# Weight loads and a stage's last outputs ahead in the engines' queues, at the seams of a one-core transformer kernel

## Chip, cores and metric

One core of a Trainium2 chip (trn2). The time is device microseconds (us) of one execution of the kernel; less is better. The time before is the median of three runs.

## What is computed

Two blocks on `x` of 512 positions by 1024 channels, in float32. Cut to what matters here:

```python
def _rms_norm(x, g):
    return x * rsqrt(mean(x * x, axis=-1) + EPS) * g

def _swiglu(x, w_gate, w_up, w_down):
    return (silu(x @ w_gate) * (x @ w_up)) @ w_down      # 1024 -> 2816 -> 1024

# first block, layers 0 and 1 (mixer: attention in layer 0, mLSTM in layer 1)
hf = _swiglu(_rms_norm(x, g[0]), ...)
x = x + 0.5 * _rms_norm(hf, g[1])
x = x + _rms_norm(mixer(_rms_norm(x, g[2])), g[3])
hf = _swiglu(_rms_norm(x, g[4]), ...)
x = x + 0.5 * _rms_norm(hf, g[5])

# second block: even mixer (pooling and a state space scan), odd mixer (gated convolution)
x = x + even_mixer(_rmsnorm(x, even_norm))
x = x + odd_mixer(_rmsnorm(x, odd_norm))
return _rmsnorm(x, final_norm)
```

What counts for the change: between two stages there is always a norm over the channels of the stage's output, an addition to x, and a norm of the new x ahead of the next stage.

## The kernel before

**Stages.** The program runs nine stages in a row: ffn0, attn, ffn1, ffn2, mlstm, ffn3, even, odd, and the final norm. Where one stage ends and the next begins is called a seam here. x is held transposed, as eight tiles (`x_91` to `x_98`) of 128 channels by 512 positions; the 512 positions are worked on in two halves of 256 columns, so that the second half's work in one stage runs beside the first half's chain on x.

**Linears.** For precision each linear is three matmuls per tile of 128 input channels (`mm3`, L280 to L290): the weight's low part times the high part of x (L287), the weight's high part times the low part of x (L288), high times high (L289). The high and low parts of x are the tiles `xs_99` to `xs_106`. A weight tile comes by `wload` (L260 to L269): an SP queue DMA into `wt` (L264), a cast into `wh` on ACT (L267), and the subtraction that leaves `wl` on DVE, or on POOL for some linears (L268). Each of the three has four buffers, so a load waits until an older tile's matmuls are done.

**End of a stage.** The last four linears run half by half (`halves`), in an ffn the very last two by `last_two` (L350 to L369), which loads two of the first linear's three weight parts a second time. Each output is evacuated from its PSUM bank on ACT by `PostNorm.evac`: its square into `ew` (L530) and its value times the gain into `yf`, `hn` or `x` (L531). The square is added to `acc` on POOL, the last of a half on DVE (L535). When a half is complete, `finish` starts a chain of small steps for it.

**The chain on x.** Per half: column sums of `acc` by matmuls with ones (L407 acc), the inverse root (`rsv`: DVE L427, POOL L428), its spread over the partitions (L415). Then for each of the eight tiles the output times the root (DVE L551), the addition to x (L553, on DVE, two of eight on POOL), the split into high (ACT L469) and low (DVE L470), the square (ACT L451) and its sum (L453 on DVE and POOL, the last L455 on DVE). Then column sums again (L407 ssq), the inverse root (`rc`: L427, L428), its spread (L415) and a copy (`rb`, L487). The matmuls of the next stage's linears need only the split of x; the factor `rb` is multiplied in when their result leaves its bank (L573 in an ffn, L700 in attn). There are four such banks, so PE can run up to four linears ahead of the end of the chain, and then waits.

**What sets the order.** The Python code yields pieces of the chains between pieces of the linears; a scheduler then gives every engine one queue in fixed order. `k.ahead(n)` raises the priority of what is written inside it, as if it had been written up to n instructions earlier. `k.chains` holds the chains that aren't finished.

Of the kernel before, what the change touches and what calls it, by code (L numbers as in the profile page):

```python
# [9 lines left out]
F32 = mybir.dt.float32  # L10
R = mybir.dt.float32r
AF = mybir.ActivationFunctionType
ALU = mybir.AluOpType
# [6 lines left out]
HALF = 256  # L20
# [121 lines left out]
class K:  # L142
# [60 lines left out]
    def evac(s, f, c0, c1):  # L203

        s.held.append((f, c0, c1))
        s.settle()
# [53 lines left out]
def wload(k, src, shape, eng=None):  # L260

    nc = k.nc
    wt = k.wp.tile(shape, F32, name="wt", tag="wt", bufs=4)
    nc.sync.dma_start(wt, src)  # L264
    wh = k.wp.tile(shape, R, name="wh", tag="wh", bufs=4)
    wl = k.wp.tile(shape, R, name="wl", tag="wl", bufs=4)
    nc.scalar.copy(wh, wt)  # L267
    (eng or nc.vector).tensor_tensor(wl, wt, wh.bitcast(F32), op=ALU.subtract)  # L268
    return wh, wl  # L269


# [21 lines left out]
class Lin:  # L293
# [12 lines left out]
    def load_part(s, i):  # L306
        src, n = s.parts[i]
        s.w[i] = wload(s.k, src, [P, n, P], s.eng)
# [44 lines left out]
def last_two(k, l0, l1, on_half):  # L353


    l0.run(*HALVES[0])
    l1.run(*HALVES[0])
    l0.w = [None, None, l0.w[2]]
    on_half(*HALVES[0])
    ps = k.A_()  # L360
    l0.part(ps, 2, *HALVES[1], True, False)
    with k.ahead(80):
        l0.load_part(0)
    l1.run(*HALVES[1])
    with k.ahead(80):
        l0.load_part(1)
    l0.part(ps, 0, *HALVES[1], False, False)
    l0.part(ps, 1, *HALVES[1], False, True)
    k.evac(lambda: l0.evac(ps, *HALVES[1]), *HALVES[1])  # L369
    on_half(*HALVES[1])  # L370


class LinTok:
# [5 lines left out]
    def run(s, tb):  # L379
        if s.w is None:  # L380
            s.w = [wload(s.k, s.src[:, 2 * kc:2 * kc + 2, :], [P, 2, T], s.eng) for kc in range(4)]
        mm = s.k.nc.tensor.matmul
        s.k.need("xs", tb * P, (tb + 1) * P)
        ps = s.k.A_()
        t = slice(tb * P, (tb + 1) * P)
        for i in range(KX):
            wh, wl = s.w[i // 2]
            xh, xl = s.xs[i]
            mm(ps, xl[:, t], wh[:, i % 2, :], start=i == 0, stop=False)
            mm(ps, xh[:, t], wl[:, i % 2, :], start=False, stop=False)  # L390
            mm(ps, xh[:, t], wh[:, i % 2, :], start=False, stop=i == KX - 1)
            s.k.tick()
        s.k.evac(lambda: s.evac(tb, ps), tb * P, (tb + 1) * P)
# [121 lines left out]
class PostNorm:  # L515
# [7 lines left out]
    def evac(s, m):  # L523
        def f(ps, c0, c1):
            k, nc = s.k, s.k.nc
            first, last = s.acc is None, c1 - c0 < T and len(s.done[c0]) == KX - 1
            if first:
                s.acc = k.sm.tile([P, T], F32, name="acc", tag="acc", bufs=1)
            sq = s.acc if first else k.ew()
            nc.scalar.activation(sq[:, c0:c1], ps[:, c0:c1], AF.Square)  # L530
            nc.scalar.activation(s.hf[m][:, c0 // HALF:c1 // HALF, :], ps[:, c0:c1].rearrange("p (a t) -> p a t", t=HALF),  # L531
                                 AF.Copy, scale=s.gain[:, m:m + 1])
            if not first:
                eng = nc.vector if last else nc.gpsimd
                eng.tensor_tensor(s.acc[:, c0:c1], s.acc[:, c0:c1], sq[:, c0:c1], op=ALU.add)  # L535
            for a, b in HALVES:
                if c0 <= a and b <= c1:
                    s.done[a].append(m)
        return f
# [18 lines left out]
def ffn(k, w, gpost, side=None, begin=None):  # L558
# [4 lines left out]
    with k.phase("ffn") as pool, k.psum("ffn_ps", True), ExitStack() as late:  # L563
# [57 lines left out]
        for m in range(KX):  # L621
            src = k.A["wd"][w, m]
            lins.append(Lin(k, [(src[:, a:b], b - a) for a, b in ((0, 8), (8, 16), (16, 22))], hs, post.evac(m)))
        run_lins(lins[:-2])
        last_two(k, *lins[-2:], post.finish)


# [1024 lines left out]
```

## Time and profile before

| | |
|---|---|
| median of three runs | 2566.19 us (2565.17 to 2567.06) |
| profiled execution | 2566.05 us |
| its span | 2564.3 us |
| mean granted clock of TensorE | 0.987 of full speed |
| PE busy | 2465.5 us, 96% of the span |
| DVE busy | 1363.8 us, 53% |
| ACT busy | 1000.4 us, 39% |
| POOL busy | 634.1 us, 25% |

PE is TensorE, DVE is VectorE, ACT ScalarE, POOL GpSimd, SP SyncE, whose queue issues the loads. The profile is of one execution; its times are us from the start of the span. Busy shares are means over all stages; a seam is a few us of 2564.

### The profile page before, as it was taken

How to read it: one execution, taken by the hardware profiler on the slowest of the kernel's cores; microseconds unless marked ns; L12 is line 12 of the kernel's file. 1: busy time of each engine (PE TensorE's matmuls, PEld its weight loads, DVE VectorE, ACT ScalarE, POOL GpSimd, SP SyncE). 2: the span in 40 equal slices, each digit the busy share in tenths (PEclk: the TensorE clock that was granted, in tenths of full speed). 3: DMA queues.
4: the chain of work that ended last, by engine and by line, in shares of the span. 5: the costliest groups of instructions: out<-in, count | busy, mean ns of one | idle time of the engine just before them, and what ended most of it. 6: DMA issues, size and time to landing. Idle time of an engine off the chain costs nothing. (4 is left out here: it accounts for less than half of the span.)

```text
span 2564.3 us, 33234 instructions
## 1 busy us (share of the span) xinstructions
PE 2465.5 (96%) x12960; PEld 2072.1 (81%) x12960; DVE 1363.8 (53%) x2298; ACT 1000.4 (39%) x1659; POOL 634.1 (25%) x560
## 2 busy tenths in 40 slices
PE   8999999999999999999999999999899999999897
PEld 7888887677888888888888888888788888787677
DVE  5344247656544432643422567558963246856885
ACT  5222235446532222422222454453222233346662
POOL 2111013030311110211100344032211015317961
PEclk9999999999999999999999999999999999999898
DMA  4323324122232333222233222223433345231211
GB/s 160 99 99 102 116 87 145 50 87 66 76 106 99 98 121 101 84 99 99 97 123 101 87 83 75 74 71 123 161 130 122 97 133 201 84 112 66 66 50 58
DMA packets 90125, 256.85 MB, mean 100 GB/s; under 512 B 16192, under 2 KB 25024, under 8 KB 89456
## 3 DMA queue, kind: packets, MB, share of 16 engines
q1 hardware_dynamic: 89968, 254.73, 31.1%
q8 instruction: 102, 1.67, 0.3%
q14 instruction: 55, 0.45, 0.1%
HBM read 229.50 MB, written 12.60 MB: 94 GB/s over the span
## 5 line engine op out<-in xcount | busy, mean ns | idle before, releaser
L287 PE MATMUL pa<-xs,wl 128*128 128x512 f32 (+1 forms) x2304 | 864.5, 375 | 25.2 <-DVE identr L243 7.9
L288 PE MATMUL pa<-xs,wh 128*128 128x512 f32 (+1 forms) x2304 | 861.7, 374 | 0.8 <-DVE xs L1423 0.6
L289 PE MATMUL pa<-xs,wh 128*128 128x512 f32 (+1 forms) x2304 | 859.6, 373 | 0.0
L267 ACT CAST wh<-wt 128x1024 fp32r<-128x1024 f32 (+2 forms) x418 | 428.0, 1025 | 978.4 <-issue 581.6
L268 DVE TENSOR_TENSOR wl<-wt,wh 128x1024 fp32r<-128x1024 f32 (+1 forms) x374 | 454.7, 1216 | 436.8 <-ACT wh L267 435.7
L287 PEld LDWEIGHTS pa<-xs,wl 128*128 128x128 f32 x2304 | 437.9, 190 | 101.8 <-ACT xs L469 13.8
L288 PEld LDWEIGHTS pa<-xs,wh 128*128 128x128 f32 x2304 | 437.9, 190 | 74.8 <-DVE xs L1423 2.5
L289 PEld LDWEIGHTS pa<-xs,wh 128*128 128x128 f32 x2304 | 438.0, 190 | 74.0 <-issue 1.8
L575 POOL TENSOR_TENSOR ew<-ew,rb 128x512 f32<-128x512 f32 (+1 forms) x96 | 159.9, 1666 | 724.9 <-ACT ew L574 724.9
L287 PE MATMUL pa<-hh,wl 128*128 128x512 f32 (+1 forms) x880 | 309.0, 351 | 4.1 <-DVE wl L268 4.1
L289 PE MATMUL pa<-hh,wh 128*128 128x512 f32 (+1 forms) x880 | 307.9, 350 | 0.0
L288 PE MATMUL pa<-hl,wh 128*128 128x512 f32 (+1 forms) x880 | 307.9, 350 | 0.0
L535 POOL TENSOR_TENSOR acc<-acc,ew 128x512 f32<-128x512 f32 (+1 forms) x46 | 56.9, 1238 | 548.3 <-ACT ew L530 548.0
L287 PEld LDWEIGHTS pa<-hh,wl 128*128 128x128 f32 x880 | 165.5, 188 | 29.1 <-DVE wl L268 4.9
L288 PEld LDWEIGHTS pa<-hl,wh 128*128 128x128 f32 x880 | 165.5, 188 | 24.3
L582 DVE TENSOR_TENSOR ew<-ew,pa 128x512 f32<-128x512 f32 (+1 forms) x96 | 61.6, 642 | 232.1 <-PE pa L289 223.1
L289 PEld LDWEIGHTS pa<-hh,wh 128*128 128x128 f32 x880 | 165.5, 188 | 23.9
L573 DVE TENSOR_TENSOR ew<-rb,pa 128x512 f32<-128x512 f32 (+1 forms) x96 | 61.6, 642 | 173.1 <-PE pa L289 172.2
L268 POOL TENSOR_TENSOR wl<-wt,wh 128x1024 fp32r<-128x1024 f32 x44 | 106.7, 2437 | 111.2 <-ACT wh L267 111.1
L1505 POOL TENSOR_TENSOR tp<-tp 128x512 f32<-128x512 f32 x72 | 99.9, 1388 | 5.1 <-ACT tp L1501 0.7
L1512 DVE SCALAR_TENSOR_TENSOR pc<-g,vecs,pc 128x512 f32<-128x512 f32 x120 | 85.8, 751 | 5.4 <-PE pc L1510 4.3
L469 ACT ACTIVATE xs<-x,vecs 128x256 fp32r<-128x256 f32 x128 | 61.0, 504 | 61.1 <-DVE x L553 41.3
(516 smaller groups left out, 2967.5 us busy)
## 6 DMA issues: line engine op xcount, KB each, us to landing
wt<-in_wgu_dram SPq DMA_DIRECT2D x176, 512.0 KB, 3.5
wt<-in_wd_dram SPq DMA_DIRECT2D x72, 512.0 KB, 3.5
wt<-in_wd_dram SPq DMA_DIRECT2D x32, 384.0 KB, 3.1
wt<-in_ow_dram SPq DMA_DIRECT2D x24, 512.0 KB, 3.2
wt<-in_aqk_dram SPq DMA_DIRECT2D x18, 512.0 KB, 4.0
xs<-x SPq DMA_DIRECT2D x32, 256.0 KB, 2.3
wt<-in_mvo_dram SPq DMA_DIRECT2D x16, 512.0 KB, 3.7
wt<-in_mqk_dram SPq DMA_DIRECT2D x16, 512.0 KB, 3.2
```

Of the source, the lines that this page charges most:

```text
L267: nc.scalar.copy(wh, wt)
L268: (eng or nc.vector).tensor_tensor(wl, wt, wh.bitcast(F32), op=ALU.subtract)
L287: mm(ps[:m, c0:c1], wl[:, j, :], xh[:, c0:c1], start=first and j == 0, stop=False)
L288: mm(ps[:m, c0:c1], wh[:, j, :], xl[:, c0:c1], start=False, stop=False)
L289: mm(ps[:m, c0:c1], wh[:, j, :], xh[:, c0:c1], start=False, stop=last and j == n - 1)
L469: nc.scalar.activation(xh[:, c0:c1], k.x[i][:, c0:c1], AF.Copy, scale=k.vec(g, i))
L535: eng.tensor_tensor(s.acc[:, c0:c1], s.acc[:, c0:c1], sq[:, c0:c1], op=ALU.add)
L573: nc.vector.tensor_tensor(s[:, c0:c1], rb[:, c0:c1], ps[:, c0:c1], op=ALU.mult)
L575: nc.gpsimd.tensor_tensor(s[:, c0:c1], s[:, c0:c1], rb[:, c0:c1], op=ALU.mult)
L582: nc.vector.tensor_tensor(s[:, c0:c1], s[:, c0:c1], ps[:, c0:c1], op=ALU.mult)
L1505: nc.gpsimd.tensor_tensor(part, part, t, op=ALU.add)
L1512: nc.vector.scalar_tensor_tensor(ps, gi[:, j:j + T], cw[:, at[j]:at[j] + 1], ps, op0=ALU.mult, op1=ALU.add)
```

## The change

Three edits. In `wload`, what is issued for a weight tile (the DMA, the cast, the subtraction) gets `k.ahead(250)` while a chain is unfinished, and stays at its place otherwise. In `last_two`, the `ahead(80)` around the two loads goes, since `wload` has its own now. In `PostNorm.evac`, the square, the scaled value and the addition to `acc` get `ahead(250)` while a chain is unfinished.

```diff
 def wload(k, src, shape, eng=None):
 
     nc = k.nc
-    wt = k.wp.tile(shape, F32, name="wt", tag="wt", bufs=4)
-    nc.sync.dma_start(wt, src)
-    wh = k.wp.tile(shape, R, name="wh", tag="wh", bufs=4)
-    wl = k.wp.tile(shape, R, name="wl", tag="wl", bufs=4)
-    nc.scalar.copy(wh, wt)
-    (eng or nc.vector).tensor_tensor(wl, wt, wh.bitcast(F32), op=ALU.subtract)
+    with k.ahead(250 if k.chains else 0):
+        wt = k.wp.tile(shape, F32, name="wt", tag="wt", bufs=4)
+        nc.sync.dma_start(wt, src)
+        wh = k.wp.tile(shape, R, name="wh", tag="wh", bufs=4)
+        wl = k.wp.tile(shape, R, name="wl", tag="wl", bufs=4)
+        nc.scalar.copy(wh, wt)
+        (eng or nc.vector).tensor_tensor(wl, wt, wh.bitcast(F32), op=ALU.subtract)
     return wh, wl
...
     l0.part(ps, 2, *HALVES[1], True, False)
-    with k.ahead(80):
-        l0.load_part(0)
+    l0.load_part(0)
     l1.run(*HALVES[1])
-    with k.ahead(80):
-        l0.load_part(1)
+    l0.load_part(1)
...
             sq = s.acc if first else k.ew()
-            nc.scalar.activation(sq[:, c0:c1], ps[:, c0:c1], AF.Square)
-            nc.scalar.activation(s.hf[m][:, c0 // HALF:c1 // HALF, :], ps[:, c0:c1].rearrange("p (a t) -> p a t", t=HALF),
-                                 AF.Copy, scale=s.gain[:, m:m + 1])
-            if not first:
-                eng = nc.vector if last else nc.gpsimd
-                eng.tensor_tensor(s.acc[:, c0:c1], s.acc[:, c0:c1], sq[:, c0:c1], op=ALU.add)
+            with k.ahead(250 if k.chains else 0):
+                nc.scalar.activation(sq[:, c0:c1], ps[:, c0:c1], AF.Square)
+                nc.scalar.activation(s.hf[m][:, c0 // HALF:c1 // HALF, :],
+                                     ps[:, c0:c1].rearrange("p (a t) -> p a t", t=HALF), AF.Copy, scale=s.gain[:, m:m + 1])
+                if not first:
+                    eng = nc.vector if last else nc.gpsimd
+                    eng.tensor_tensor(s.acc[:, c0:c1], s.acc[:, c0:c1], sq[:, c0:c1], op=ALU.add)
```

The lines of the changed kernel from 264 to 362 stand one lower in the file than before (L268 is L269), those from some 366 to 528 one higher (L407 is L406, L427 is L426, L455 is L454).

No instruction of PE, DVE, POOL or SP comes or goes; ACT has three loads of its function tables less, all in ffn3's first part. Only the seams and the kernel's start have a new order. Two places:

DVE at the seam from attn to ffn1, from the splits of the last two x tiles of the first half (`xs6_105`, `xs7_106`) to the second half's chain. The four `wl` are the first four weight tiles of ffn1, `rsv` belongs to the second half, `rc` to the first. Before:

```order
L470 SCALAR_TENSOR_TENSOR xs6_105<-x6_97,vecs_89,xs6_105 128x256
L453 TENSOR_TENSOR ssq_5550<-ssq_5550,sq_5558 128x256
L470 SCALAR_TENSOR_TENSOR xs7_106<-x7_98,vecs_89,xs7_106 128x256
L453 TENSOR_TENSOR ssq_5550<-ssq_5550,sq_5561 128x256
L268 TENSOR_TENSOR wl_5696<-wt_5693,wh_5695 128x1024
L455 TENSOR_TENSOR ssq_5550<-ssq_5550,ssq_5542 128x256
L268 TENSOR_TENSOR wl_5804<-wt_5801,wh_5803 128x1024
L535 TENSOR_TENSOR acc_5221<-acc_5221,ew_5655 128x256
L268 TENSOR_TENSOR wl_5846<-wt_5843,wh_5845 128x1024
L427 TENSOR_SCALAR rsv_5712<-pb_5709 128x2
L427 TENSOR_SCALAR rc_5470<-pb_5721 128x2
L268 TENSOR_TENSOR wl_5881<-wt_5878,wh_5880 128x1024
```

and with the change, from the last of the four `wl` on:

```order
L269 TENSOR_TENSOR wl_5881<-wt_5878,wh_5880 128x1024
L553 TENSOR_TENSOR x7_98<-x7_98,ew_5537 128x256
L452 TENSOR_TENSOR ssq_5550<-ssq_5550,sq_5552 128x256
L535 TENSOR_TENSOR acc_5221<-acc_5221,ew_5655 128x256
L452 TENSOR_TENSOR ssq_5550<-ssq_5550,sq_5555 128x256
L469 SCALAR_TENSOR_TENSOR xs6_105<-x6_97,vecs_89,xs6_105 128x256
L426 TENSOR_SCALAR rsv_5712<-pb_5709 128x2
L469 SCALAR_TENSOR_TENSOR xs7_106<-x7_98,vecs_89,xs7_106 128x256
L452 TENSOR_TENSOR ssq_5550<-ssq_5550,sq_5558 128x256
L452 TENSOR_TENSOR ssq_5550<-ssq_5550,sq_5561 128x256
L454 TENSOR_TENSOR ssq_5550<-ssq_5550,ssq_5542 128x256
L426 TENSOR_SCALAR rc_5470<-pb_5721 128x2
```

All four `wl`, the second half's last addition to `acc` and its `rsv` now stand ahead of the first half's last step on `ssq` (L455, now L454). On PE the column sums of `acc` stood behind `xs_103`'s matmuls with those of `ssq` right behind them and `rsv`'s spread six matmuls on; with the change those of `acc` stand three matmuls earlier, and 17 matmuls lie between them and those of `ssq`, with `rsv`'s spread right behind. On ACT the four evacuation pairs of the second half stood behind the splits of `x6_97` and `x7_98` and ahead of the cast for `wl_5881`; now they stand ahead of these splits and behind that cast.

DVE at the seam from ffn0 to attn, at the end of the first half's chain; the `wl` are weight tiles of attn's first linears. Before:

```order
L268 TENSOR_TENSOR wl_3029<-wt_3026,wh_3028 128x1024
L453 TENSOR_TENSOR ssq_2717<-ssq_2717,sq_2728 128x256
L535 TENSOR_TENSOR acc_2003<-acc_2003,ew_2858 128x256
L455 TENSOR_TENSOR ssq_2717<-ssq_2717,ssq_2709 128x256
L268 TENSOR_TENSOR wl_3064<-wt_3061,wh_3063 128x1024
L427 TENSOR_SCALAR rc_2630<-pb_2832 128x2
L268 TENSOR_TENSOR wl_3070<-wt_3067,wh_3069 128x1024
L268 TENSOR_TENSOR wl_3076<-wt_3073,wh_3075 128x1024
```

and with the change:

```order
L269 TENSOR_TENSOR wl_3064<-wt_3061,wh_3063 128x1024
L469 SCALAR_TENSOR_TENSOR xs6_105<-x6_97,vecs_89,xs6_105 128x256
L535 TENSOR_TENSOR acc_2003<-acc_2003,ew_2858 128x256
L469 SCALAR_TENSOR_TENSOR xs7_106<-x7_98,vecs_89,xs7_106 128x256
L452 TENSOR_TENSOR ssq_2717<-ssq_2717,sq_2722 128x256
L656 MEMSET bt_2877 8x640
L452 TENSOR_TENSOR ssq_2717<-ssq_2717,sq_2725 128x256
L269 TENSOR_TENSOR wl_3070<-wt_3067,wh_3069 128x1024
L452 TENSOR_TENSOR ssq_2717<-ssq_2717,sq_2728 128x256
L269 TENSOR_TENSOR wl_3076<-wt_3073,wh_3075 128x1024
L454 TENSOR_TENSOR ssq_2717<-ssq_2717,ssq_2709 128x256
```

Three more `wl` stand ahead of the first half's last step. On PE the column sums of `ssq` stand 27 matmuls later. At the other seams behind an ffn `wl` move forward likewise, and ahead of the last step there are as many as before at ffn1 to ffn2 and ffn3 to even, and one more at ffn2 to mlstm, where the column sums of `ssq` stand 7 matmuls later. At mlstm to ffn3 the order changes as at attn to ffn1, and some 17 small steps of `ssm_prep` (side work of ffn3 for the even stage) move ahead of the second half's chain.

## Rows read from the trace of the kernel before

**Rows 1.** The page, part 1: busy time of each engine.
```profile
PE 2465.5 (96%) x12960; PEld 2072.1 (81%) x12960; DVE 1363.8 (53%) x2298; ACT 1000.4 (39%) x1659; POOL 634.1 (25%) x560
```
**Rows 2.** What PE waited for: us in total, times, longest us.
```profile
PE pb L407 <- DVE ssq L455: 9.8, 8, 3.8
...
PE pa L287 <- DVE ew L573: 5.3, 3, 2.7
PE pa L287 <- ACT yf L531: 4.3, 2, 3.5
...
PE pa L287 <- ACT hn L531: 3.6, 1, 3.6
...
PE pa L287 <- ACT x L531: 1.5, 1, 1.5
```
**Rows 3.** Timeline of PE: start, us, engine, line, operation, count [idle before, releaser].
```profile
380.75 0.39 PE L287 MATMUL pa<-hh,wl 128*128 128x256 f32 x1 [1.01 <-DVE wl L268]
...
673.51 0.28 PE L289 MATMUL pa<-xs,wh 128*128 128x256 f32 x1
677.33 0.36 PE L287 MATMUL pa<-xs,wl 128*128 128x256 f32 x1 [3.55 <-ACT yf L531]
...
681.46 0.68 PE L407 MATMUL pb<-ones,acc 128*128 128x128 f32 x4 [0.85 <-DVE acc L535]
681.98 0.61 PE L407 MATMUL pb<-ones,ssq 128*128 128x128 f32 x4
682.35 0.36 PE L287 MATMUL pa<-xs,wl 128*128 128x256 f32 x1
...
683.37 0.71 PE L415 MATMUL pb<-ident,rsv 128*128 128x128 f32 x4
...
694.81 0.36 PE L287 MATMUL pa<-xs,wl 128*128 128x256 f32 x1 [1.32 <-DVE ew L573]
```
**Rows 4.** Windows: stretch, length, busy us (instructions), PEclk, DMA share, GB/s.
```profile
core 0: us, PE busy (x) PEld busy (x) DVE busy (x) ACT busy (x) POOL busy (x), PEclk, DMA share, GB/s
...
1048.00:1056.00 8.00, 6.07 (x47) 5.70 (x48) 8.00 (x14) 5.06 (x10) 1.00 (x1) 1.00 0.61 198
...
380.00:388.00 8.00, 6.12 (x50) 5.95 (x50) 7.92 (x14) 5.66 (x11) 1.70 (x3) 1.00 0.59 159
...
664.80:677.10 12.30, 8.99 (x75) 8.78 (x74) 12.17 (x27) 10.79 (x25) 4.54 (x5) 1.00 0.01 1
...
677.40:682.50 5.10, 4.25 (x24) 3.99 (x25) 2.87 (x5) 1.42 (x3) 3.30 (x3) 0.67 0.62 206
...
694.80:700.80 6.00, 5.99 (x51) 6.00 (x51) 4.14 (x11) 3.82 (x7) 2.25 (x3) 1.00 0.01 1
...
1071.00:1077.00 6.00, 6.00 (x29) 6.00 (x30) 3.49 (x10) 1.45 (x4) 2.06 (x3) 0.50 0.01 3
```
**Rows 5.** Timeline of DVE, ffn0 to attn and attn to ffn1, columns as in rows 3.
```profile
394.07 0.75 DVE L551 TENSOR_TENSOR ew<-x,pb 128x256 f32<-128x256 f32 x2 [1.28 <-PE pb L415]
...
675.63 0.42 DVE L453 TENSOR_TENSOR ssq<-ssq,sq 128x256 f32<-128x256 f32 x1
675.97 1.22 DVE L268 TENSOR_TENSOR wl<-wt,wh 128x1024 fp32r<-128x1024 f32 x1
...
680.89 0.43 DVE L535 TENSOR_TENSOR acc<-acc,ew 128x256 f32<-128x256 f32 x1 [2.23 <-POOL acc L535]
...
684.12 0.42 DVE L551 TENSOR_TENSOR ew<-yf,pb 128x256 f32<-128x256 f32 x1 [0.18 <-PE pb L415]
```
**Rows 6.** Timeline of ACT and of POOL at attn to ffn1.
```profile
672.90 1.03 ACT L267 CAST wh<-wt 128x1024 fp32r<-128x1024 f32 x1
...
675.26 0.36 ACT L530 ACTIVATE ew<-po 128x256 f32<-128x256 f32 x1
...
675.88 0.37 ACT L530 ACTIVATE ew<-po 128x256 f32<-128x256 f32 x1
...
675.70 3.55 POOL L535 TENSOR_TENSOR acc<-acc,ew 128x256 f32<-128x256 f32 x1 [3.86 <-ACT ew L530]
```
**Rows 7.** Groups by line on DVE, ffn3's side work: busy us, mean ns, idle before.
```profile
L1121 DVE TENSOR_TENSOR pad__14064<-pa__14058,pdt 128x16 f32<-128x16 f32 x1 | 0.2, 172 | 0.0
```

## Prediction

> **What bounds the kernel now.** I read the page first: TensorE (PE) is busy 2465.5 us of a span of 2564.3, so all its idle time is 98.8 us [rows 1], and a change that moves instructions can only win from that, or from time that PE spends at its lower clock. The PE waits come next [rows 2]: each row gives what PE waited for, the total, the number of waits and the longest. Three of these rows wait for what the change takes ahead, the stage's last outputs (yf, hn and x through L531, 4.3 + 3.6 + 1.5 us). Two are ends of the chain on x: ssq (9.8) and ew L573 (5.3).
>
> Then the PE timeline at the seams, the places where one stage ends and the next begins. In each of the four seams behind an ffn PE waits about 1.01 us for the weights that `last_two` loads; one row stands for the four, 1.01, 1.01, 1.01 and 1.02 [rows 3]. At attn to ffn1 it stops for 3.55 us, at mlstm to ffn3 for 3.6 (the hn row), at ffn1 to ffn2 for 1.5 (the x row) [rows 2, 3]. Together the front waits are 4 x 1.01 + 3.55 + 3.6 + 1.5 = 12.7 us, which is the most the change could take away by itself.
>
> The windows decide the argument [rows 4]. In the seam at ffn1 to ffn2 VectorE (DVE) is busy 8.00 of 8.00 us, at ffn0 to attn 7.92 of 8.00, and ahead of attn to ffn1's stop 12.17 of 12.30, while PE has holes. It does the chain on x (adds, splits, squares' sums) and the wl subtractions in one queue. PE's front wait is the sight of a full DVE queue: what is taken ahead there pushes something else behind.
>
> **The change part by part.** It adds and removes no instruction on PE and DVE; it moves some. The prices are a wl at 1.22 us, a chain step at 0.42, an evacuation pair (L530, L531) at 0.62 (675.26 to 675.88 for the next pair's start), a wh cast at 1.03 [rows 5, 6].
>
> *Weight loads ahead, at the four seams behind an ffn.* One wl goes ahead of chain steps that stood before it, so PE's 1.01 us goes: 4 x 1.01 = 4.0 us at the front. But the first half's last step L455, for which PE waits next (the ssq row: 9.8 - 3.8 over the other 7 waits is 0.86 us each [rows 2]), stands behind as many wl as before at ffn1 to ffn2 and at ffn3 to even, with a DVE that never pauses. It ends when it did, and PE, 1.01 us further, waits that much longer at L407. Net 0 at these two; only if L455 isn't what decides could 1.01 be kept, which is the other bound. At ffn0 to attn three more wl go ahead of L455 (3 x 1.22 = 3.66 us later). PE doesn't ask then: its L407 was moved behind 27 matmuls of 0.12 us (51 in 6.00 us at full clock [rows 4]), 3.2 us. The second half's chain started at 394.07 after 1.28 us in which DVE had nothing [rows 5]; that slack takes most of it. Bounds: the 1.01 kept, or 3.66 - 1.28 - 1.01 = 1.4 lost; I take 0, the middle nearly. At ffn2 to mlstm it is one more wl (1.22) and 7 matmuls; bounds 1.01 kept or 0.4 lost, 0 taken. The SP queue's loads go ahead too, by a few DMAs; they wait for a buffer, not the queue, so nothing.
>
> *Last outputs ahead, at ffn1 to ffn2.* PE's 1.5 us at the front can go. Then L407 on ssq waits for the rest, since L455 doesn't come earlier; after that the second half's chain is as before, and PE's longest wait for ew L573, 2.7 us [rows 2], ends when that chain does. 0, bounds 0 to 1.5 won.
>
> *attn to ffn1, step by step.* On ScalarE (ACT) the four evacuation pairs go ahead of the last two splits, but the cast wh of the fourth load now stands ahead of them, and I take it that its buffer comes free with the last matmul before the stop, which ends at 673.51 + 0.28 = 673.79 [rows 3]. So 673.79 + 1.03 + 3 x 0.62 = 676.68 for the third pair, which gives PE its bank, and PE went on at 677.33: it wins some 0.6 of the 3.55 here. On POOL the first add into acc took 3.55 us [rows 6], and all three were done 2.23 us after DVE's run of instructions had ended, at 680.89 - 2.23 = 678.66 [rows 5]: they ran when DVE paused. By that row they run now when DVE reaches acc and waits: the fourth wl to 674.82 + 1.22 = 676.04, then two steps at 0.34 from start to start (675.63 to 675.97 [rows 5]), 676.7; + 2.23 gives 678.9, DVE's own add and L407 0.57 later 679.5, against 681.46 [rows 3]: 2 us earlier. Then it is lost again, on PE: from L407 on acc to the broadcast of rsv there were 6 matmuls and the L407 on ssq, now there are 17 and the L407 on ssq, which in turn needs L455, now behind all four wl. 679.5 + 0.52 for L407 (681.46 to 681.98 [rows 3]), 17 matmuls, 0.37 for L407 on ssq (to 682.35) and 0.75 from L415 to L551 [rows 3, 5]: with the matmuls at the 0.21 us of half the clock (29 in 6.00 us [rows 4]) 684.7, at 0.12 683.2, and at the mean granted clock of this stretch, 0.67 [rows 4], 0.18 x 17 = 3.1 and 684.2, against 684.12 now. The second half's chain of some 10 us (L551 at 684.12 [rows 5]) sets when PE's bank comes free at 694.81 [rows 3]. So the seam ends between 1.0 us earlier and 0.6 later; I take the middle, 0.2 earlier. What PE no longer waits at 677.33 and 681.46 it waits at 694.81.
>
> The Trainium skill says of this port (SBUF — State Buffer, section "SBUF: two separate sides") that DVE and GpSimd share a port pair as an exclusive lock, and the second to come blocks until the holder's instruction is done. Here the row says more: blocked through four DVE instructions in a row, not one. By the page's rule the adds would slip in behind single instructions, the two steps of 0.34 wouldn't hold them, and each of the two such seams would come out another 0.7 us earlier, the sum 1.4 lower; I go by the row.
>
> *mlstm to ffn3* has the same waits (3.6 in front, 5.3 - 2.7 - 1.32 = 1.3 at the rear [rows 2, 3]) and the same moves: 0.2. About 17 small DVE steps of `ssm_prep` (0.17 us each by the row of L1121 [rows 7]), 2.9 us together, now come ahead of the second chain; DVE's wait of 2.2 us for POOL, and those for PE behind it, hide most of them. *Start of the kernel:* a few wl and the first column sums change places, where PE waits for the first loads either way: 0.
>
> **Sum.** -0.2 - 0.2 = -0.4 on the profiled execution, 2566.05 (span 2564.3 and 1.75 around it): 2565.65. The median of the three runs lies 0.14 above it, so I forecast 2565.8. This case's own range, from the bounds (won: 4.0 + 1.5 + 2 x 1.0 = 7.5; lost: 1.4 + 0.4 + 2 x 0.6 = 3.0), is 2558.5 to 2569.
>
> **Rivals.** *The front gains stay.* For it: PE's idle time at the fronts is large, 12.7 us, and the half-speed stretch behind the stop, 5.10 us at 0.67, costs 1.7 us at each of two seams. Then 2566.2 - 12.7 - 3.4 = 2550 in full; without the 2.9 us by which the evacuations can't move, twice, 2556. It needs DVE to have air in the seams, for instance because the order of before let it wait on ACT. Against it: DVE's 8.00 of 8.00 [rows 4].
>
> *The wait merges and the clock pays: slower.* PE's waits go from the front to the rear, in one piece. Behind the 1.32 us at 694.81 PE stays at full clock (1.00), behind the 2.7 at ffn1 to ffn2 (ended just ahead of 1071) it runs 6 us at 0.50, 1.2 instead of 2.4 GHz, which costs 3.0 us [rows 4]. If at attn to ffn1 0.6 + 0.85 + 1.32 = 2.8 us [rows 3] are waited at the rear, and the same at mlstm to ffn3, each costs 3.0: +6.0 - 0.4, 2571.8; with one more seam behind an ffn, where 1.01 and 0.86 become one wait of 1.9, 2574.8. [...] Against it: matmuls in that stretch lean on the chain only at the bank, and the half clock behind the front stop would go in exchange.
>
> *It does not do what it says.* A row's place in a queue is changed, but where it waits for a DMA or a buffer nothing starts earlier. Then the time is 2566.2, inside the forecast's case.
>
> **How the numbers follow.** A measurement can tell 0.2%, 5.1 us: faster is below 2561.1, slower above 2571.3. My forecast's case has 0.50 and the change that does nothing 0.10, of which together 0.04 lies under 2561.1 and 0.56 within; gains that stay 0.25; merged waits 0.15, of which 0.01 stays within. So faster 0.29, same 0.57, slower 0.14. The range leaves out the full gain below and the third slow seam above: 2554 to 2573.
>
> **What would show it.** Right: PE's waits for wl in the four ffn seams and for yf and hn shrink in the changed profile, and those for ssq L455 and ew L573 grow by as much; L551 of the second half starts within 1 us of 684.12 at attn to ffn1; acc on DVE ends near 679 there. Wrong: PE's idle time falls by 5 us or more in all, or DVE has holes in the windows of the seams, or the granted clock behind 694.81 falls to 0.50.

## The result and the profile after

The changed kernel takes **2584.3 us** (median of four runs, 2583.9 to 2587.48) against 2566.36 of the kernel before in the same runs (2565.17 to 2567.06): a ratio of 1.0074 [1.0062, 1.0086], 18 us slower. The forecast was 2565.8 with a range of 2554 to 2573; the result lies outside it, on the side that had 0.14.

The page of the changed kernel, part 1, answers to [rows 1]:

```profile
PE 2470.8 (96%) x12960; PEld 2077.4 (80%) x12960; DVE 1367.0 (53%) x2298; ACT 997.6 (39%) x1656; POOL 628.1 (24%) x560
```

The span is 2582.9, so PE's idle time is 112.1 us (98.8 before): 13.3 of the 18.6 us are waits, and 5.3 us are more busy time for the same 12960 matmuls, that is, time at a lower clock (the mean granted clock is 0.984; it was 0.987).

What PE waited for, in the changed kernel, us in total, times, longest (answers to [rows 2]):

```profile
PE pb L406 <- DVE ssq L454: 22.2, 7, 12.6
...
PE pa L288 <- DVE ew L573: 6.6, 3, 2.8
...
PE pb L406 <- DVE acc L535: 5.1, 2, 4.7
...
PE pa L288 <- ACT hn L531: 3.7, 1, 3.7
...
PE pa L288 <- DVE wl L269: 1.1, 1, 1.1
...
PE pa L288 <- ACT yf L531: 0.8, 1, 0.8
```

The change did at the fronts what it says: the four waits for `last_two`'s wl behind an ffn are gone, and the stop for yf at attn to ffn1 with them (4.3 to 0.8). The row of these wl before was:

```profile
PE pa L287 <- DVE wl L268: 5.7, 6, 1.1
```

But one wait of 12.6 us for ssq is new. It stands at mlstm to ffn3. The timelines of PE, DVE and ACT there, in the changed kernel (columns as in [rows 3]):

```profile
1731.39 0.77 PE L406 MATMUL pb<-ones,ssq 128*128 128x128 f32 x2 [12.61 <-DVE ssq L454]
```
```profile
1730.71 0.20 DVE L1192 TENSOR_SCALAR pc__14173<-pc__14173 128x64 f32<-128x64 f32 x1 [13.42 <-DMA pc__14173<-in_sc_dram]
1730.83 0.42 DVE L454 TENSOR_TENSOR ssq<-ssq 128x256 f32<-128x256 f32 x1
```
```profile
1728.86 1.28 ACT L1119 ACT_TABLE_LOAD   x1 [12.96 <-DMA pdt<-in_ldt_dram]
```

DVE's queue is in order. L1192, a 0.20 us step of ffn3's side work (`ssm_prep`), now stands directly ahead of L454, the last step of the first half's ssq. It waits 13.42 us for a transfer, and L454, whose inputs were there at 1717.2 when the sum ahead of it was done, waits behind it; PE waits for L454, and the linears behind these column sums in PE's queue wait too. ACT's queue stands as well, 12.96 us for pdt (the log_dt of `ssm_prep`), with the splits of the second half behind it.

Why is the transfer late? The SP queue, which issues the loads, first in the kernel before, then in the changed one (start, us from the start of the first to the end of the last of the row, line, tile, count):

```profile
1667.74 15.74 SPq L264 DMA_DIRECT2D wt<-in_wgu_dram  x4
...
1684.01 1.39 SPq L1117 DMA_DIRECT2D pdt<-in_ldt_dram  x2
...
1690.62 2.86 SPq L1178 DMA_DIRECT2D pc__14173<-in_sc_dram  x1
```
```profile
1701.99 3.84 SPq L265 DMA_DIRECT2D wt<-in_wgu_dram  x2
...
1706.36 1.38 SPq L1117 DMA_DIRECT2D pdt<-in_ldt_dram  x2
1709.34 3.33 SPq L265 DMA_DIRECT2D wt<-in_wgu_dram  x1
1712.71 7.71 SPq L1127 DMA_DIRECT2D pskip<-in_sd_dram  x1
1720.52 4.94 SPq L1176 DMA_DIRECT2D pb__14171<-in_sb_dram  x1
1725.56 0.57 SPq L1178 DMA_DIRECT2D pc__14173<-in_sc_dram  x1
```

Before, four of ffn3's weight loads stood ahead of the small loads of `ssm_prep`; now there are six, and the last two, issued between 1701.99 and 1705.83, wait for a buffer (each tile has four). So pdt is issued at 1706.36 instead of 1684.01, and pc at 1725.56 instead of 1690.62; of the 22 us by which pdt is later, 4.3 are what the changed kernel had lost until then (table below). pc is another 12.6 us later than that: one more weight load stands between, and behind the slow loads the issue of pskip lasts 7.71 us and that of pb 4.94 (4.41 and 0.57 before). The view of DMA issues says how long they take to land (KB each, median us), first before, then changed:

```profile
pdt<-in_ldt_dram SPq DMA_DIRECT2D x2, 4.0 KB, 13.6
```
```profile
pdt<-in_ldt_dram SPq DMA_DIRECT2D x2, 4.0 KB, 21.7
...
pskip<-in_sd_dram SPq DMA_DIRECT2D x1, 8.0 KB, 17.5
...
wt<-in_wgu_dram SPq DMA_DIRECT2D x4, 512.0 KB, 3.3
```

Two loads of 4 KB take 21.7 us where 512 KB take 3.3, and the 8 KB issued after them take 17.5. pdt's source has every second number of a short list, spread over 64 partitions: single numbers. In the kernel before they are slow as well (13.6 us, and 20.2 for pskip behind them), but lay beside other work.

Behind the stop, a window of the changed kernel (columns as in [rows 4]):

```profile
1731.40:1737.40 6.00, 6.00 (x28) 6.00 (x29) 4.27 (x19) 1.53 (x6) 1.60 (x2) 0.50 0.03 8
```

PE runs six us at 0.50 of its clock, 1.2 GHz, which costs 3.0. The wait for acc in front is 1.00 us shorter than before (0.37 instead of 1.37). The wait for ew L573 at the rear is still there, first before, then in the changed kernel:

```profile
1726.34 0.36 PE L287 MATMUL pa<-xs,wl 128*128 128x256 f32 x1 [1.31 <-DVE ew L573]
```
```profile
1745.28 0.35 PE L288 MATMUL pa<-xs,wl 128*128 128x256 f32 x1 [1.52 <-DVE ew L573]
```

Together 12.6 + 3.0 - 1.0 + 0.2 is 14.8 us. The same weight cast on ACT started 4.3 us later than in the kernel before ahead of this seam and 19.0 behind it, a step of 14.7, which agrees.

### The profile page after: what moved, and what is told of

Its sections match the earlier page's. It is cut to its first block, busy times and chain, and to the rows that moved or that the text cites. A ratio compares the mean times of both kernels' runs of the same rounds, so it can differ in the third digit from the quotient of the medians.

```text
span 2582.9 us, 33246 instructions
## 1 busy us (share of the span) xinstructions
PE 2470.8 (96%) x12960; PEld 2077.4 (80%) x12960; DVE 1367.0 (53%) x2298; ACT 997.6 (39%) x1656; POOL 628.1 (24%) x560
## 2 busy tenths in 40 slices
DMA packets 90125, 256.85 MB, mean 99 GB/s; under 512 B 16192, under 2 KB 25024, under 8 KB 89456
## 5 line engine op out<-in xcount | busy, mean ns | idle before, releaser
L268 ACT CAST wh<-wt 128x1024 fp32r<-128x1024 f32 (+2 forms) x418 | 428.0, 1025 | 972.9 <-issue 589.4
L269 DVE TENSOR_TENSOR wl<-wt,wh 128x1024 fp32r<-128x1024 f32 (+1 forms) x374 | 458.0, 1225 | 437.2 <-ACT wh L268 436.1
L535 POOL TENSOR_TENSOR acc<-acc,ew 128x512 f32<-128x512 f32 (+1 forms) x46 | 51.2, 1113 | 549.3 <-ACT ew L530 549.0
L573 DVE TENSOR_TENSOR ew<-rb,pa 128x512 f32<-128x512 f32 (+1 forms) x96 | 61.6, 641 | 174.6 <-PE pa L290 173.7
L269 POOL TENSOR_TENSOR wl<-wt,wh 128x1024 fp32r<-128x1024 f32 x44 | 106.7, 2438 | 108.7 <-ACT wh L268 108.7
```

What stands on the lines that cost most here:

```text
L573: nc.vector.tensor_tensor(s[:, c0:c1], rb[:, c0:c1], ps[:, c0:c1], op=ALU.mult)
```

## Experiments

Every run was made beside runs of the kernel before (medians 2565.65, 2565.43 and 2565.75). Two theories at first. *One seam:* all of the loss is the late side work at mlstm to ffn3. *Everywhere:* at every seam what is taken ahead pushes the chain back, with a lower clock behind (the rival of the prediction). Edits are against the changed kernel unless it says otherwise.

### x1: the order of before at one seam

```diff
-    with k.ahead(250 if k.chains else 0):
+    with k.ahead(250 if k.chains and not k.off else 0):   # also in evac
...
+        k.off = True       # ahead of mlstm's output linears
...
+        k.off = False      # behind ffn3's first four linears
```

> The change everywhere but at the seam from mlstm to ffn3, where loads and last outputs keep their place of before. Both theories that put the loss at this one seam (the small loads of ssm_prep come late; or the DVE order there costs) expect 2566.4 + about 4 = 2570, with PE's 12.6 us wait for ssq gone, and the stop at attn to ffn1 as in the changed kernel (some 2 us later than before). If every seam pays through the clock, as my third case had it, it stays above 2576.

Measured: 2573.62 (2572.55 to 2575.9), ratio 1.0033 [1.0021, 1.0045], between the two figures expected. Each against the kernel before in its own runs, the changed kernel loses 17.9 us and x1 8.0, so the seam accounts for 10.0. *One seam* is not the whole: 8 us remain in other places.

### x2: the small loads at the start of the kernel

```diff
+    k.side = [k.const.tile([P, 2, 16], F32, name="pa_"), k.const.tile([P, 16], F32, name="pdt"),
+              k.const.tile([P, 16], F32, name="pskip")]
...
+    with k.ahead(400):
+        nc.sync.dma_start(a, A["sa"])
...
```

The small loads for seven tiles, `pb` and `pc` of the first two rounds among them, go into tiles of their own and are issued near the start.

> The change everywhere, but ssm_prep's first seven small loads go to buffers of their own and are issued near the start of the kernel, so that no weight load stands ahead of them; the 17 or so small DVE steps still stand ahead of the second half's chain at mlstm to ffn3. Late loads theory: the 12.6 us wait goes, 2570 to 2572. DVE order theory (the steps and four wl ahead of the last step on ssq cost by themselves): 2580 to 2584.

Measured: 2582.03 (2580.08 to 2583.32), 1.0062 [1.0047, 1.0077]. In the whole this missed, and it lies in the range of the rival, the order on DVE. The trace says otherwise: the 12.6 us wait is gone (the longest for ssq is 3.7) and the seam costs some 3 us instead of 14.7 by the weight casts around it, with more small steps ahead of the chain than in the changed kernel. But the slow loads now stand ahead of ffn0's weights. The timelines of SP and PE in this run:

```profile
18.18 2.84 SPq L1120 DMA_DIRECT2D pdt<-in_ldt_dram  x2
```
```profile
46.39 0.50 PE L291 MATMUL pa<-xs,wl 128*128 128x512 f32 x1 [4.76 <-DVE wl L272]
```

PE waits there for weights, and by 90 us the kernel is 8.2 us behind the kernel before (the changed one 2.0). The queue was blocked elsewhere.

### x3 and x4: one part of the change alone

x3 has only the `ahead` in `wload` (and `last_two` without its own), x4 only that in `PostNorm.evac`, with loads as before:

```diff
-            with k.ahead(250 if k.chains else 0):     # x3: evac as before
...
-    with k.ahead(250 if k.chains else 0):             # x4: wload as before
+    with k.ahead(80):                                 # x4: last_two, twice
```

> wload's part of the change alone (with last_two's); last outputs keep their place. Late loads theory: the SP queue still has two more weight loads ahead of ssm_prep's, and a step that needs one stands on DVE ahead of the second chain, so most of the loss stays, 2578 to 2585. If it is the last outputs that upset the seams: 2566 to 2570.

Measured: 2588.64 (2586.33 to 2592.09), 1.009 [1.0075, 1.0105], above the expectation.

> The last outputs' part of the change alone; loads as before. Late loads theory: ssm_prep's loads pa and pdt stand where they stood, its DVE steps behind the second half's chain, no long wait at mlstm to ffn3: 2564 to 2569. If it is the last outputs that upset the seams: above 2575.

Measured: 2570.43 (2567.35 to 2573.44), 1.0016 [1.0006, 1.0026], just above it. So the loads cost more than the whole change, and the outputs, a loss alone, win 4 to 5 us back beside them. x3 has the same wait in the DVE waits:

```profile
DVE pc__14173 L1191 <- DMA pc__14173<-in_sc_dram: 13.4, 1, 13.4
```

### x5 and x6: the slow load made short

log_dt comes from the host laid out for the tile, and the two loads of single numbers become one of 8 KB; x5 is the changed kernel with this, x6 the kernel before with it. Nothing else is moved: in x5 only a few small side steps of DVE and POOL behind L454 stand elsewhere than in the changed kernel, in x6 none.

```diff
-    A["ldt"] = np.ascontiguousarray(I["ssm_log_dt_2"][0])
+    A["ldt"] = np.ascontiguousarray(np.repeat(I["ssm_log_dt_2"][0].reshape(16, 2).T, 64, axis=0))
...
-    ld = A["ldt"].rearrange("(q two) -> two q", two=2)
-    for gg in range(2):
-        nc.sync.dma_start(dt[gg * 64:(gg + 1) * 64, :], ld[gg:gg + 1, :].to_broadcast([64, 16]))
+    nc.sync.dma_start(dt, A["ldt"])
```

> The change everywhere, but ssm_prep's log_dt comes from a table laid out as [128, 16] in one load of 8 KB instead of two loads of single numbers, which took 21.7 us from issue to landing. The places in the queues stay as in the changed kernel. Late loads theory, with the slow loads as the part that hurts: pc lands near 1718 instead of 1730.7, the wait for ssq at mlstm to ffn3 falls from 12.6 us to at most 2, the kernel to 2571 to 2575. If the SP queue's place alone (two weight loads that wait for buffers ahead) makes the delay: the wait stays above 6 us, 2578 to 2584.

> The kernel before with the same short load of log_dt. There the slow loads are issued 22 us earlier, ahead of the seam, and nobody waits: 2563 to 2567, no difference that can be told. If the kernel before already paid for them, it comes out 2 us or more faster.

Measured: x5 2574.71 (2571.92 to 2576.55), 1.0034 [1.0021, 1.0048]; x6 2566.55, 1.0001 [0.9991, 1.001]. Both as expected. SP, DMA issues and DVE in x5:

```profile
1710.32 0.42 SPq L1115 DMA_DIRECT2D pdt<-in_ldt_dram  x1
1710.79 0.43 SPq L1125 DMA_DIRECT2D pskip<-in_sd_dram  x1
...
1713.68 0.59 SPq L1174 DMA_DIRECT2D pb__14170<-in_sb_dram  x1
1714.37 0.57 SPq L1176 DMA_DIRECT2D pc__14172<-in_sc_dram  x1
```
```profile
pskip<-in_sd_dram SPq DMA_DIRECT2D x1, 8.0 KB, 2.6
```
```profile
1721.71 0.19 DVE L1190 TENSOR_SCALAR pc__14172<-pc__14172 128x64 f32<-128x64 f32 x1
1721.81 0.42 DVE L454 TENSOR_TENSOR ssq<-ssq 128x256 f32<-128x256 f32 x1
```

The scaling of pc stands at the same place ahead of L454, and pdt is issued as late as in the changed kernel (26.3 us later than before, in a trace that is 8.3 us late there), but the issues of pskip and pb last 0.43 and 0.59 us instead of 7.71 and 4.94, pskip lands in 2.6 us instead of 17.5, and neither DVE nor ACT waits for these loads. This is the run that settles the first cause: not the place of the small steps, nor their number, nor the late issue by itself, but a late issue of *slow* loads, in front of in-order queues. Where they are early, the same load costs nothing (x6). x5 changes the layout and the number of loads together, and doesn't tell the two apart.

### x7 and x8: the rest, by place

x7 has the change at the four seams behind an ffn alone, x8 at two of them (ffn0 to attn, ffn1 to ffn2).

```diff
-    with k.ahead(250 if k.chains else 0):
+    with k.ahead(250 if k.chains and k.on else 0):   # also in evac
...
+        k.on = w in (0, 1, 2, 3)      # x8: (0, 1); ahead of last_two
```

> The change only at the four seams behind an ffn; the start, attn to ffn1 and mlstm to ffn3 as before. From the changed kernel's trace, seam by seam: ffn0 to attn 1.1 won, ffn1 to ffn2 0.5 won, ffn2 to mlstm 1.8 lost, ffn3 to even 0.6 lost: 2565.7 + 0.8, so 2565 to 2568. If the seams depend on what came before them, up to 2572.

> The change only at ffn0 to attn and ffn1 to ffn2, the two seams that came out shorter in the changed kernel's trace: 1.6 won, 2564, or no difference that can be told (2562 to 2567). If what was won there was only catching up what the start and attn to ffn1 had lost: 2566 to 2568.

Measured: x7 2573.63 (2571.46 to 2576.62), 1.0031 [1.002, 1.0042]; x8 2574.69 (2572.58 to 2575.57), 1.0033 [1.0021, 1.0044]. Both missed. I had expected most of the rest at attn to ffn1, which x7 leaves as before; x7 has all of it, 8.2 us. x8 doesn't divide the seams, and the fault is in its edit: at the two other seams it also lacks the `ahead(80)` of before, and PE waits longer at their fronts than the 1.01 and 1.02 of before. PE in x8:

```profile
1433.63 0.39 PE L289 MATMUL pa<-hh,wl 128*128 128x256 f32 x1 [2.50 <-DVE wl L270]
...
2110.94 0.39 PE L289 MATMUL pa<-hh,wl 128*128 128x256 f32 x1 [4.16 <-DVE wl L270]
```

The page of x7 says that its 7.3 us more of span (2571.6) are 2.8 us of idle time and 4.5 us of busy time (x6, with the order of before, has 0.6 us more busy time):

```profile
PE 2470.0 (96%) x12960; PEld 2076.2 (81%) x12960; DVE 1364.3 (53%) x2298; ACT 1000.9 (39%) x1659; POOL 634.5 (25%) x560
```

PE at ffn2 to mlstm in x7, all its waits between 1437 and 1446:

```profile
1438.98 0.50 PE L390 MATMUL pa<-wl,xs 128*128 128x512 f32 x1 [1.24 <-DVE wl L270]
...
1440.79 0.68 PE L407 MATMUL pb<-ones,ssq 128*128 128x128 f32 x4 [1.08 <-DVE ssq L455]
...
1442.88 0.71 PE L415 MATMUL pb<-ident,rc 128*128 128x128 f32 x4 [0.49 <-POOL rc L428]
...
1445.07 0.71 PE L415 MATMUL pb<-ident,rsv 128*128 128x128 f32 x4 [0.56 <-POOL rsv L428]
```

The 1.01 us at the front is gone; now PE stands for wl of the next stage, then at three links of the chain in a row.

### x9 and x10: the rest, by part

As x7, but x9 with the loads alone and x10 with the outputs alone.

```diff
-            with k.ahead(250 if k.chains else 0):     # x9: evac
+            with k.ahead(0):
...
-    with k.ahead(250 if k.chains else 0):             # x10: wload
+    with k.ahead(0):
...
+    with k.ahead(80):                                 # x10: last_two, as before
```

> wload's part of the change alone, and only at the four seams behind an ffn. If the wl that go ahead there push the chain steps that PE waits for next (ssq, rc, rsv, one behind the other), the 8 us that the four seams cost with both parts (2573.6) come from this part: 2571 to 2575. If the last outputs are what costs there: 2565 to 2568.

> The last outputs' part alone, and only at the four seams behind an ffn; loads as before. Only the place of some 25 rows of DVE and 15 of PE changes. Loads theory: 2564 to 2567, no difference that can be told. Outputs theory: 2571 or more.

Measured: x9 2577.91 (2575.61 to 2579.6), 1.0045 [1.003, 1.006], above its range; x10 2569.16 (2565.76 to 2572.53), 1.0011 [1.0002, 1.0021], between its two ranges. At the ffn seams too the loads are the loss, 12 us, and the outputs win some 4 of it back. PE at ffn1 to ffn2 in x9, and the window behind:

```profile
1056.63 0.58 PE L289 MATMUL pa<-xs,wl 128*128 128x256 f32 x1 [4.85 <-ACT x L532]
```
```profile
1056.60:1062.60 6.00, 5.81 (x26) 5.61 (x26) 2.34 (x8) 0.42 (x1) 0.63 (x1) 0.53 0.41 137
```

The wait for the last outputs, 1.5 us before [rows 2], is 4.85 with the loads ahead of them, and behind it PE goes on at 0.53 of its clock. In the changed kernel, where the outputs go ahead as well, it is 2.0. The outputs alone don't shorten it; PE in x10:

```profile
1055.42 0.38 PE L289 MATMUL pa<-xs,wl 128*128 128x256 f32 x1 [1.50 <-ACT x L534]
```

### x11 and x12: a shorter way, and a longer one for two loads

x11 is x5 with 80 in place of 250; x12 is the kernel before with 250 in place of 80 in `last_two`.

```diff
-    with k.ahead(250 if k.chains else 0):      # x11, both places
+    with k.ahead(80 if k.chains else 0):
...
-    with k.ahead(80):                          # x12, against the kernel before
+    with k.ahead(250):
```

> The change everywhere with 80 queued instructions in place of 250, and with the short load of log_dt. If the number of steps that a load overtakes sets the cost, less is lost than with 250 and the short load (2574.7): 2567 to 2572. If any move of the loads in a full DVE queue costs as much: 2573 to 2576.

> The kernel before with 250 in place of 80 at last_two's two loads, nothing else: PE's first wait of 1.01 us at the four seams behind an ffn goes, and only the two loads overtake anything. If that wait is given back in the chain, 2564.5 to 2567; if the later loads are the ones that hurt, and these two help, 2561.5 to 2564.

Measured: x11 2568.16 (2562.25 to 2569.89), 1.0004 [0.9995, 1.0014]; x12 2570.28 (2567.68 to 2573.93), 1.0018 [1.0008, 1.0028], which is above both figures expected: no change, or a small gain. With 80 most of the remaining loss is gone, but x11 can't be told from no change. Taking just the two loads of `last_two` further ahead costs 4.5 us. None of the twelve kernels beats the one before; x6 equals it.

### Where the time is lost, over the span

The start of the same ACT cast of a weight, us later than in the kernel before, at seven times of its trace:

| in the middle of | ffn0 | attn's end | ffn1 | ffn2 | mlstm's end | ffn3 | even |
|---|---|---|---|---|---|---|---|
| changed | 2.0 | 0.9 | 3.1 | 2.6 | 4.3 | 19.0 | 19.5 |
| x1 | 1.0 | 0.7 | 3.5 | 3.1 | 4.8 | 5.2 | 7.6 |
| x5 | 1.2 | 3.7 | 7.0 | 5.4 | 8.3 | 7.9 | 10.5 |
| x7 | 1.4 | 3.6 | 4.8 | 4.6 | 6.7 | 6.2 | 7.9 |
| x6 (order of before) | -0.2 | -1.7 | -0.5 | -2.9 | -2.8 | -2.5 | -1.9 |

The step of 14.7 us at mlstm to ffn3 stands out and is absent in x1, x5 and x7. By the medians the seam is worth less, 10.0 us by x1 and 8.7 by x5. The changed kernel and x5 have the same order up to mlstm's end, and there their traces are 4.0 us apart (4.3 and 8.3); one trace against another is no better than that, and where the rest of the 14.7 us goes stays open. The other steps of 1 to 3 us are no larger than x6, which moved nothing, differs from the kernel before, so a single trace can't say which ffn seam holds how much of the 8 us; only the medians of x7, x9 and x10 carry that part. One small step repeats, though: from ffn2 to mlstm's end all four traces with the change lose 1.7 to 2.9 us and x9 (loads alone) 3.5, but x6 0.1, x4 0.5 and x10 0.4 (outputs alone in both).

## Why the prediction was wrong

**The SP queue, the step that failed.** "The SP queue's loads go ahead too, by a few DMAs; they wait for a buffer, not the queue, so nothing." The premise was right and the conclusion wrong. Just because two more weight loads wait for a buffer, the queue holds what stands behind them: pdt is issued 22 us later. I hadn't asked what that is and who waits for it. The price, put at nothing, is 10.0 us by x1 and 8.7 by x5.

**The small steps.** "About 17 small DVE steps ... DVE's wait of 2.2 us for POOL, and those for PE behind it, hide most of them." Their busy time is hidden indeed: x5 has them at the same places ahead of L454, and the seam costs nothing by its trace. What I left out is what they wait for. A step of 0.20 us whose operand is late costs the wait, and all of it lands on the chain behind.

**The four seams behind an ffn: "0 taken".** PE's front wait of 1.01 us is gone at all four, and more than that is lost behind it: my bounds came to 1.8 us lost in all (1.4 and 0.4), and x7 gives 8.2 us for the four. I counted only the wl ahead of L455. With the loads ahead PE also waits longer for the last outputs (4.85 us in x9, 2.0 with the outputs ahead as well) and for later wl (1.24 in x7), and I had priced no clock there.

**ffn1 to ffn2: "0, bounds 0 to 1.5 won".** The wait for x became longer, 2.0 us, not shorter. Outputs alone leave it at 1.50 (x10), loads alone make it 4.85 (x9): the outputs alone won nothing here, and the loads made a loss of which the outputs win back a part.

**attn to ffn1: -0.2, bounds -1.0 and +0.6.** The front stop of 3.55 us went, as forecast (PE busy 2.38 of 3.40 us in the window from 674.0). DVE's addition to acc came at 680.88, not near 679. PE in the changed kernel there, answering to [rows 3]:

```profile
681.44 1.19 PE L406 MATMUL pb<-ones,acc 128*128 128x128 f32 x4 [4.74 <-DVE acc L535]
...
686.05 0.67 PE L406 MATMUL pb<-ones,ssq 128*128 128x128 f32 x4
686.56 0.61 PE L414 MATMUL pb<-ident,rsv 128*128 128x128 f32 x4
```

The waits of 3.55 and 0.85 have become one of 4.74, the 17 matmuls ran at a low clock (0.60 in the window from 681.4 to 687.4), and L551 of the second half starts at 687.21 instead of 684.12. Less the 0.9 us by which the changed kernel was late already, the bank comes free some 2.2 us later. By the medians this seam can't be told from 0: x7, with the order of before there, is no faster than x1, which has the change there (2573.63 and 2573.62).

**mlstm to ffn3: "the same waits and the same moves".** Not the same: the front stop stayed, 3.71 us for hn (3.6 before). Of the two waits in front only that for acc shrank, 1.37 to 0.37, and the one at the rear grew from 1.31 to 1.52.

**The rule I went by on POOL.** I let POOL's additions run "when DVE pauses", by [rows 6]. In the changed kernel POOL and DVE at attn to ffn1 show otherwise:

```profile
677.41 3.26 POOL L535 TENSOR_TENSOR acc<-acc,ew 128x256 f32<-128x256 f32 x3 [2.75 <-ACT ew L530]
```
```profile
677.52 1.70 DVE L269 TENSOR_TENSOR wl<-wt,wh 128x1024 fp32r<-128x1024 f32 x1
679.14 0.95 DVE L553 TENSOR_TENSOR x<-x,ew 128x256 f32<-128x256 f32 x1
680.01 0.94 DVE L452 TENSOR_TENSOR ssq<-ssq,sq 128x256 f32<-128x256 f32 x1
680.88 0.41 DVE L535 TENSOR_TENSOR acc<-acc,ew 128x256 f32<-128x256 f32 x1
```

The three additions went through beside a busy DVE, whose steps took 0.95 us instead of 0.42 and whose wl took 1.70 instead of 1.22. The Trainium skill (SBUF — State Buffer, section "SBUF: two separate sides") lets either engine block the other for one instruction; these rows agree with that, and the 3.55 us of before, through four instructions, are left unexplained by it. No run here tells the two apart further.

**The rivals.** "The wait merges and the clock pays" gave 2574.8 with three seams, near what is left without the slow load (2574.71). Its mechanism shows in part: a merged wait and a low clock at attn to ffn1 and in x9. Its place doesn't: the rear wait at attn to ffn1 was 2.27 us, and behind it the clock stayed at full speed, the changed kernel's window from 698:

```profile
698.00:704.00 6.00, 6.00 (x51) 6.00 (x52) 4.15 (x11) 3.73 (x6) 2.08 (x3) 1.00 0.01 1
```

Its price, 3.0 us of clock for a wait of 2.7, was read from one row. In x6, with the order of before, the same wait is followed by full clock; PE and the window behind:

```profile
1070.33 0.36 PE L287 MATMUL pa<-xs,wl 128*128 128x256 f32 x1 [2.70 <-DVE ew L573]
```
```profile
1070.30:1076.30 6.00, 5.87 (x47) 5.72 (x48) 4.62 (x11) 2.65 (x6) 2.30 (x3) 1.00 0.01 3
```

So the length of one wait doesn't say what the clock will cost, and that 2574.8 came near is luck.

No rival of mine had the 10 us of the late side work in it. How much of the other 8 us is the clock alone stays open: PE's busy time rose by 4.5 us in x7, and the mean granted clock is 0.984 to 0.986 over its eight runs (0.986 to 0.989 in the runs of before beside them), but no run kept PE busy during those waits, nor was the slow load made late in the kernel before without the rest of the change.

**The signs named ahead.** Of those of being right, L551 at attn to ffn1 (687.21) and the end of acc there (681.29) failed. Of those of being wrong, one came: DVE had a hole of 13.42 us in a seam. PE's idle time rose instead of falling, and the clock behind attn to ffn1's rear wait stayed at 1.00.

## What to carry to other kernels

When work goes ahead in an engine's queue, read what it passes on *every* queue it is issued to, the DMA queue too, and follow the transfers that now start later to the first instruction that needs them and to what stands behind that one. A load that takes long and is hidden is safe only while it is early; make it short before you let anything pass it. An engine that is busy all through a seam gives nothing for an earlier start: two loads taken further ahead lost 4.5 us in all (x12).

## What was not expected of the hardware

Two loads of 4 KB of single numbers took 13.6 us to land in the kernel before and 21.7 in the changed one, and the next load in the queue, 8 KB, took 20.2 and 17.5 us; with the numbers laid out as the tile has them and loaded at once, that next load took 2.6. The Trainium skill (DMA: Bandwidth & Descriptors, section "Rules for kernel authors") says that a last dimension which isn't contiguous becomes one descriptor per element, and advises to rearrange. The trace agrees: x5 has 88189 DMA packets and the changed kernel 90125, all 1936 of the difference under 512 B. It adds that the loads behind pay for it too.
